# A macaron FFN–mixer–FFN layer on one core: TensorE in program order, streamed tiles moved by 64 bytes, other sums of squares

## The chip, the cores and the metric

The program runs on one core of one Trainium2 chip. The metric is the device time of one execution in microseconds (us), as a median of several runs. One profiled execution is read beside it; a group of rows is quoted word for word further down, and line numbers such as L351 are those of the kernel before.

## What is computed

One layer and a final norm, over 1024 tokens of width 1024 in float32, with a feed-forward width of 2816:

```
x = x + 0.5 * SwiGLU_1(RMSNorm(x))
x = x + W_out concat[ GLA heads(RMSNorm(x)), short-conv groups(RMSNorm(x)) ]
x = x + 0.5 * SwiGLU_2(RMSNorm(x))
out = RMSNorm(x)

rmsnorm(x, g):  x * rsqrt(mean(x * x) + 1e-6) * g
swiglu(x):      (silu(x @ w_gate) * (x @ w_up)) @ w_down
```

## The kernel before, in words

**Layout.** x lies transposed in SBUF as eight tiles of 128 channels by 1024 tokens, and the tokens are taken in two halves of 512 columns. Each operand of a product is split into two reduced float32 parts, high and low (`split`: a cast on ScalarE, then a subtraction on VectorE), and each product is three passes on TensorE (high by high, high by low, low by high), so that nearly all of TensorE's work is matmuls of 128x128 weights by 512 columns.

**FFN.** The 2816 hidden channels are 22 blocks f of 128 (gate and up together). Blocks 0 and 1 are done by `plain` as ordinary products. Blocks 2 to 21 go through a scheme of seven products in place of eight (`ups`, in the order u1, u5, u6, u2, u7, u3, u4; 12 matmuls each), and after each even f the pair of blocks before it is multiplied into x by `down` (D1, D2, D6, D3, D7, D5, D4). One period, two `ups` and one `down`, is 7x12x2 + 84 = 252 matmuls; each FFN has ten. The streamed right operands of `ups` are tiles named R (R11, R12, R21, R22 and S1, in pools with the tag R or h) and S (S2, S3, S4, in a pool of their own, `side`); of the seven products of one `ups` four stream an R tile and three an S tile, so 72 matmuls of a period have the form `ps<-S,w`. Sums between the products run on VectorE: after u7, `add(V, u1, ...)` (the row `act<-ps,p`, L88) reads the PSUM bank into which u4 then goes on accumulating, so u4 can start only behind it. The last pair is multiplied by `down_last` (L601), over ranges of tokens, and after each block d of a range the callback `after(n, d)` takes the square for the next norm.

**Weights** come in by DMA on SyncE's queue and are split by ScalarE and VectorE, some after a sum on GpSimd; `pump`, `free` and `need` move these steps along as room comes free, and `tick` and `spawn` place the norm's steps, written as generators, between the products by a count of TensorE's time.

**Norm.** `Norm.add(k)` squares a tile on ScalarE and adds it to a running sum; `stat` is four small matmuls (L314) that sum over the partitions, `fin` makes the reciprocal root (pow on GpSimd, L328), a diagonal `dg` on VectorE (L331), the broadcast matmul `rb` (L335), and, with `keep`, a copy of it to SBUF. `raw` (L342) multiplies x by gain and root. n1 and n3 are the norms ahead of the FFNs, n2 that ahead of the mixer, n4 the last one, which has three ranges in `tail`: 512, 256 and 256 tokens.

**Seams.** Seam 1 is the stretch from the first `down_last` to the mixer's first projections (`alr`, L709, and `pj`, L691), seam 2 that from the mixer's output projection (`dn`, L996) to the second `plain` (L461).

**Order.** A scheduler orders each engine's instructions by its own priorities within the dependences. `in_order(since)` adds dependences that keep every engine to program order; before, it is called once, at the start, over the first half of the first norm.

**Addresses.** Pools are laid one behind the other. By their sizes S3, S4 and S2 begin at 101376, 117760 and 134144 bytes in each partition, which are multiples of 128, as is the mixer's tile `o` of the second half. R, h, act, w and the mixer's `z` begin 64 bytes over a multiple of 128.

Of the kernel before, what the change touches and what calls it, by code (L numbers as in the profile page):

```python
# [16 lines left out]
P = 128  # L17
# [38 lines left out]
def trunk(ctx: ExitStack, tc: tile.TileContext, a, out):  # L56
# [220 lines left out]

    def rstd_of(ss, n):

        ms = tiny.tile([P, 4], F32, tag="ms", name=nm("ms"))  # L280
        G.tensor_scalar_add(ms[:, :n], ss[:, :n], EPS)
        r = tiny.tile([P, 4], F32, tag="rs", name=nm("rs"))
        G.tensor_tensor(r[:, :n], ms[:, :n], nhalf[:, :n], op=ALU.pow)
        return r

    class Norm:


        def __init__(self, c, w=HALF, engines="VGVGVVV"):
            self.c, self.w, self.n, self.engines, self.sums = c, w, w // P, engines, []  # L290
# [9 lines left out]
        def add(self, k):  # L300

            q, sums = self.square(k), self.sums
            two = "V" in self.engines
            if k < 1 + two:
                sums.append(q)
                return
            i = k % 2 if two and k < 6 else 0
            add(V if self.engines[k - 1] == "V" else G, sums[i], sums[i], q)
            if two and k == 6:
                add(V, sums[0], sums[0], sums.pop())  # L310
# [5 lines left out]
        def fin(self, bank, st=None, keep=True):  # L316

            n = self.n
            ss = tiny.tile([P, 8], F32, tag="st", name=nm("ss"))
            if st is None:  # L320
                t = bank("st")
                self.stat([t[:, 2 * j:2 * j + 2] for j in range(n)], self.sums[0], True, True)
                V.tensor_scalar_add(ss[:, 0:2 * n], t[:, 0:2 * n], EPS)
            else:
                for j in range(n):
                    V.tensor_scalar_add(ss[:, 2 * j:2 * j + 2], st[j], EPS)
            r = tiny.tile([P, 4], F32, tag="rs", name=nm("rs"))
            G.tensor_tensor(r[:, :n], ss.rearrange("p (j c) -> p j c", c=2)[:, :n, 0], nhalf[:, :n], op=ALU.pow)  # L328
            yield 4.0
# [3 lines left out]
            yield 1.5  # L333
# [3 lines left out]
            if keep:  # L337
                self.r = t2("rb")[:, :self.w]
                S.copy(self.r, rp)

# [16 lines left out]
    class Ffn:  # L357
# [81 lines left out]
        def half1_end(self):  # L439
            for q in range(2):  # L440
                self.right(("S3", "S4")[q], ("S3", "S4")[q])
                for k in range(4):
                    self.part(("S3", "S4")[q], k, self.raws[q, k])
            self.raws.clear()
# [6 lines left out]
        def plain(self):  # L451
            for n in range(2):
                for f in range(2):
                    pss = [self.bank(4 * n + 2 * f + m) for m in range(2)]
                    for q in range(2):
                        lts = [need(((self.i, "f", f), f"L{m + 1}{q + 1}")) for m in range(2)]
                        for k, rk in enumerate(self.r_of(f"R{q + 1}{n + 1}")):
                            for m in range(2):
                                for t, (i, j) in enumerate(PASSES):
# [3 lines left out]
                                                     stop=(q == 1 and k == 3 and t == 2))  # L463
                        if q:
# [6 lines left out]
                        tick(5.44)  # L471
# [112 lines left out]
        def down_last(self, after, ranges):  # L584
# [5 lines left out]
            for n, (c, w) in enumerate(ranges):  # L590
                h, o = divmod(c, HALF)
                for d in range(KT):
# [12 lines left out]
                    after(n, d)  # L605
                    tick(1.36 * w / HALF)
            free("wo", 4)


        def run(self, after, shut, ranges):  # L610
            self.plain()
            for _ in self.side:
                pass
            self.half1_end()
# [9 lines left out]
            shut()  # L624
            self.down_last(after, ranges)
# [381 lines left out]
    def norm_h(norm, h, bank):  # L1007

        yield from norm.fin(bank)
# [9 lines left out]
    def in_order(since):  # L1019

        prev = {}
        for i in nc.cur_bb.bb.instructions[since:]:
            if i.engine in prev:
# [3 lines left out]
        return len(nc.cur_bb.bb.instructions), prev  # L1027
# [32 lines left out]
    st = [f1.bank(4 + j)[:, 0:2] for j in range(4)]  # L1060
# [7 lines left out]
    pump(2)  # L1068
    pump(2)
# [3 lines left out]
    start = in_order(0)  # L1073
    for k in range(KT):
        nc.sync.dma_start(out=xh(k, 1), in_=a["x"][k * P:(k + 1) * P, HALF:T])
    nc.sync.dma_start(out=w_a1, in_=a["w_a1"])
# [148 lines left out]
```

## Time and profile before

| | before |
|---|---|
| median of 3 runs (lowest, highest) | 1829.99 us (1827.4, 1830.26) |
| the profiled execution | 1829.83 us |
| its span, first to last instruction | 1828.0 us, so 1.83 us lie around it |
| TensorE's mean granted clock | 0.983 of full speed |
| VectorE, ScalarE, GpSimd busy | 77%, 45%, 36% of the span |
| loads of weights and x | 107 MB, 61 GB/s over the span |

A row of the timeline or of a group names line, engine, operation and tiles (out<-in), then how many; in brackets stands the idle time before it and what ended that. Matmuls overlap in the pipeline, so the step from one start to the next tells what a matmul costs, and the printed duration (some 390 ns) does not.

### The profile page before, as it was taken

The page shows a single profiled execution, that of the slowest core. Times are in us where ns is not written, and L with a number is a line of the kernel's source. Part 1 is how long each engine was busy: PE and PEld are TensorE (multiplying, and loading weights), DVE is VectorE, ACT ScalarE, POOL GpSimd, SP SyncE. Part 2 cuts the span into 40 slices and gives each one's busy share as a digit, 9 for nine tenths or more (in the row PEclk, how much of TensorE's full clock was granted, in tenths as well). Part 3 has the DMA queues.
Part 4 walks back from the last instruction along what each step waited for, and adds up shares of the span by engine and source line. Part 5 has one row for each costly group of instructions (what it writes and reads, how often), then busy time and mean ns, then how long its engine had stood idle before and what let it go on. Part 6 is the DMA issues. An engine that isn't in the chain of part 4 may idle for free.

```text
span 1828.0 us, 20978 instructions
## 1 busy us (share of the span) xinstructions
PE 1761.6 (96%) x7830; PEld 1431.9 (78%) x7830; DVE 1405.9 (77%) x1822; ACT 814.3 (45%) x1432; POOL 650.1 (36%) x441
## 2 busy tenths in 40 slices
PE   8899999999999997899999999999999999999995
PEld 6678877878778876688888887877877887787874
DVE  4687888878887886666655668797888788887887
ACT  4354444544454453523343444454445444454442
POOL 2442445335442445120120121343544244533531
PEclk9899999999999998999999999999999999999997
DMA  5002111111112121222222222111111212111102
GB/s 187 24 24 70 52 63 48 46 58 58 47 46 70 49 73 35 69 84 84 76 78 84 93 70 81 43 39 58 58 47 47 70 48 65 50 47 58 58 24 92
DMA packets 35302, 112.92 MB, mean 62 GB/s; under 512 B 4576, under 2 KB 7040, under 8 KB 35200
## 3 DMA queue, kind: packets, MB, share of 16 engines
q1 hardware_dynamic: 35200, 111.58, 18.4%
q8 instruction: 61, 1.00, 0.2%
q14 instruction: 41, 0.34, 0.1%
HBM read 107.37 MB, written 4.19 MB: 61 GB/s over the span
## 4 chain that ended last, share of the span: by engine, by line
PE 68%; DVE 25%; issue 2%; POOL 2%; ACT 2%; DMA 0%; ACTq 0%; DVEq 0%; POOLq 0%
PE ps L351 37%; PE pj L691 11%; DVE x L519 8%; DVE act L85 5%; PE dn L996 5%; DVE w L85 5%; PE ps L581 3%; PE ps L461 2%; PE ps L601 2%; PE v L746 2%; DVE T L85 2%; POOL hraw L85 2%; DVE hraw L342 2%; PE sc L815 1%; PE ps L314 1%
## 5 line engine op out<-in xcount | busy, mean ns | idle before, releaser
L351 PE MATMUL ps<-R,w 128*128 128x512 f32 x1920 | 463.4, 391 | 3.0 <-DVE w L85 2.4
L351 PEld LDWEIGHTS ps<-R,w 128*128 128x128 f32 x1920 | 358.7, 188 | 88.3 <-DVE w L85 11.4
L581 PE MATMUL ps<-act,w 128*128 128x512 f32 x1680 | 400.2, 391 | 7.6 <-ACT ps L550 7.6
L581 PEld LDWEIGHTS ps<-act,w 128*128 128x128 f32 x1680 | 313.8, 188 | 81.2 <-ACT ps L550 16.0
L351 PE MATMUL ps<-S,w 128*128 128x512 f32 x1440 | 352.1, 397 | 4.1 <-ACT ps L493 4.1
L85 DVE TENSOR_TENSOR w<-raw,w 128x512 fp32r<-128x512 f32 x316 | 292.1, 926 | 54.0 <-ACT w L92 53.9
L351 PEld LDWEIGHTS ps<-S,w 128*128 128x128 f32 x1440 | 271.6, 189 | 71.0 <-ACT ps L493 5.0
L85 POOL TENSOR_TENSOR raw<-raw 128x512 f32<-128x512 f32 x60 | 78.4, 1307 | 642.4 <-DVE w L85 642.4
L92 ACT CAST w<-raw 128x512 fp32r<-128x512 f32 x316 | 194.9, 619 | 165.7 <-POOL raw L85 92.8
L88 POOL TENSOR_TENSOR x<-x,dx 128x512 f32<-128x512 f32 x160 | 264.1, 1686 | 7.2 <-ACT dx L568 7.2
L519 DVE SCALAR_TENSOR_TENSOR x<-ps,x 128x512 f32<-128x512 f32 x320 | 207.1, 684 | 49.3 <-PE ps L581 49.3
L691 PE MATMUL pj<-h,whi 128*128 128x512 f32 x640 | 201.9, 396 | 0.0
L85 DVE TENSOR_TENSOR wlo<-raw,whi 128x1024 fp32r<-128x1024 f32 x64 | 82.3, 1285 | 89.1 <-PE pj L691 52.8
L691 PEld LDWEIGHTS pj<-h,whi 128*128 128x128 f32 x640 | 119.7, 190 | 26.6 <-issue 1.9
L85 DVE TENSOR_TENSOR w<-T,w 128x512 fp32r<-128x512 f32 x120 | 118.3, 986 | 22.0 <-ACT w L92 22.0
L218 ACT CAST whi<-raw 128x1024 fp32r<-128x1024 f32 x64 | 67.0, 1047 | 138.1 <-PE pj L691 79.8
L691 PE MATMUL pj<-h,wlo 128*128 128x512 f32 x320 | 125.4, 392 | 0.0
L92 ACT CAST w<-T 128x512 fp32r<-128x512 f32 x120 | 74.3, 619 | 94.3 <-DVE T L85 56.2
L85 DVE TENSOR_TENSOR act<-act,act 128x512 fp32r<-128x512 f32 x98 | 103.2, 1054 | 13.5 <-ACT act L92 13.5
L92 ACT CAST act<-act 128x512 fp32r<-128x512 f32 x98 | 61.1, 626 | 116.6 <-DVE act L505 64.8
L85 DVE TENSOR_TENSOR T<-raw,raw 128x512 f32<-128x512 f32 x60 | 63.2, 1054 | 55.8 <-POOL raw L85 55.8
L85 POOL TENSOR_TENSOR raw<-raw,raw 128x512 f32<-128x512 f32 x60 | 97.9, 1631 | 4.7
(170 smaller groups left out, 2137.5 us busy)
## 6 DMA issues: line engine op xcount, KB each, us to landing
raw<-in_ffn_w SPq DMA_DIRECT2D x88, 512.0 KB, 3.5
raw<-in_ffn_wd SPq DMA_DIRECT2D x44, 512.0 KB, 3.5
raw<-in_w_fm SPq DMA_DIRECT2D x40, 512.0 KB, 3.4
raw<-in_w_out SPq DMA_DIRECT2D x16, 512.0 KB, 3.4
x<-in_x SPq DMA_DIRECT2D x16, 256.0 KB, 5.7
raw<-in_w_v SPq DMA_DIRECT2D x8, 512.0 KB, 3.4
out<-y SPq DMA_DIRECT2D x8, 256.0 KB, 2.1
out<-y SPq DMA_DIRECT2D x16, 128.0 KB, 2.0
```

Source lines behind the costliest of these rows:

```text
L85: eng.tensor_tensor(o, x, y, op=ALU.subtract)
L88: eng.tensor_tensor(o, x, y, op=ALU.add)
L92: S.copy(hi, src)
L218: S.copy(st[1], st[0])
L342: V.scalar_tensor_tensor(o, self.x(k), gains[:, g, k:k + 1], self.r, op0=ALU.mult, op1=ALU.mult)
L351: nc.tensor.matmul(ps, lt[:, c:c + P], rk[j], start=(start and n == 0), stop=(n == last), skip_group_check=True)
L461: nc.tensor.matmul(pss[m], lts[m][:, c:c + P], rk[j], start=(q == 0 and k == 0 and t == 0), stop=(q == 1 and k == 3 and t == 2))
L519: V.scalar_tensor_tensor(xh(d, n), ps, 0.5, xh(d, n), op0=ALU.mult, op1=ALU.add)
L581: nc.tensor.matmul(ps, l2[i], r[0][j], start=(start and n == 0), stop=(n == 2), skip_group_check=True)
L601: nc.tensor.matmul(ps, l2[i], rts[h][q][:, 512 * j + o:512 * j + o + w], start=(q == 0 and k == 0), stop=(q == 1 and k == 2))
L691: nc.tensor.matmul(pss[f], w[i][:, k, f * P:(f + 1) * P], h[j][:, 4 * kh + k, :], start=(kh == 0 and k == 0 and n == 0), stop=(kh == 1 and ...
L996: nc.tensor.matmul(pss[j], w[p][:, f * 512 + j * P:f * 512 + (j + 1) * P], act[q][i][:, f * 512:(f + 1) * 512], start=(i == 0 and f == 0 a ...
```

## The change

It has four parts. A tile `pad` of 64 bytes is laid ahead of the `side` pools, so that all S tiles and the mixer's o tiles begin 64 bytes later. TensorE's instructions of each FFN, from `plain` to ahead of `down_last`, are kept to program order, and from `down_last` to the seam's end (the end of the program in the second FFN) all four engines are; the start's range in program order takes in the squares of the second half. The sums of squares are made otherwise: n1's first half on VectorE in place of 32 small matmuls on TensorE (64 records in the profile), n2's first half by two chains on VectorE and GpSimd in place of one on GpSimd, the last range of n4 on VectorE; n2's first half reads its root from PSUM without a copy, and `norm_h` splits each tile one step behind. At the end results are stored as pairs of tiles, on SyncE's and ScalarE's queues in turn, the first range is scaled by ScalarE and GpSimd, the others by VectorE.

```diff
+    ctx.enter_context(tc.tile_pool(name="pad", bufs=1)).tile([P, 16], F32, name="pad")
...
     class Norm:
-        def __init__(self, c, w=HALF, engines="VGVGVVV"):
+        def __init__(self, c, w=HALF, chain=None):
...
             q, sums = self.square(k), self.sums
-            two = "V" in self.engines
-            if k < 1 + two:
+            if k < 1 + (self.chain is None):
                 sums.append(q)
...
+            elif self.chain:
+                add(self.chain, sums[0], sums[0], q)
+            else:
+                i = k % 2 if k < 6 else 0
+                add((V, G)[i], sums[i], sums[i], q)
...
-        def fin(self, bank, st=None, keep=True):
+        def fin(self, bank, keep=True, waits=(2.7, 1.3), fill=lambda: None):
...
     def run(self, after, shut, ranges):
+            since = here()
             self.plain()
             for _ in self.side:
                 pass
-            self.half1_end()
+            spawn(self.half1_end())
...
             shut()
+            in_order(since, nc.tensor)
+            self.end = here()
             self.down_last(after, ranges)
...
     def norm_h(norm, h, bank, keep=True):
-        for k in range(KT):
-            raw = t2("hraw")
-            norm.raw(raw, 1, k)
-            split(raw, hi[:, k, :], lo[:, k, :])
-            if k % 2:
-                yield 2.7
+        prev = None
+        for k in range(KT + 1):
+            if k < KT:
+                raw = t2("hraw")
+                norm.raw(raw, 1, k)
+            if prev is not None:
+                split(prev, hi[:, k - 1, :], lo[:, k - 1, :])
+                yield 1.3
+            prev = raw
...
-    n1 = [Norm(0), Norm(HALF, engines="GGGGGGG")]
-    n2 = [Norm(0, engines="GGGGGGG"), Norm(HALF, engines="GGGGGGG")]
+    n1 = [Norm(0, chain=V), Norm(HALF, chain=G)]
+    n2 = [Norm(0), Norm(HALF, chain=G)]
...
-    n4 = [Norm(*r) for r in tail]
+    n4 = [Norm(*tail[0]), Norm(*tail[1]), Norm(*tail[2], chain=V)]
...
     for k in range(KT):
-        n1[0].stat(st, n1[0].square(k), k == 0, k == KT - 1)
-    begin = n1[0].fin(f1.bank_norm, st, False)
+        n1[0].add(k)
+    begin = n1[0].fin(f1.bank_norm, False)
...
     for k, _ in enumerate(f1.half0(n1[0])):
         if k >= 4:
             pump(1)
-    start = in_order(0)
+        n1[1].add(k)
+    f1.start = in_order(0, nc.tensor, V, S, G)
...
-            spawn(norm_h(n2[0], hm[0], f1.bank_norm))
+            spawn(norm_h(n2[0], hm[0], f1.bank_norm, False), 4.0)
     f1.run(to_mix, eh.close, halves)
     finish()
+    in_order(f1.end, nc.tensor, V, S, G)
...
+    def first():
+        yield from n4[0].fin(f2.bank_norm)
+        for k in range(0, KT, 2):
+            y = room("wr", "y")
+            for i in range(2):
+                xg, yv = t2("xg"), y[:, i * HALF:(i + 1) * HALF]
+                S.mul(xg, n4[0].x(k + i), gains[:, 3, k + i:k + i + 1])
+                G.tensor_tensor(yv, xg, n4[0].r, op=ALU.mult)
+            store(0, k, y.rearrange("p (i c) -> p i c", i=2))
+            yield 1.3
...
     f2.run(last, eh.close, tail)
     finish()
+    in_order(f2.end, nc.tensor, V, S, G)
```

**In the layers**, this is TensorE before, over the last two `ups` of an FFN (f odd, then f even): a row is a line, the bank written, the right operand and the weights.

```order
L351 MATMUL ps_4729<-R_189,w_4652 128x512 x11
L351 MATMUL ps_4650<-R_394,w_4631 128x512 x12
L351 MATMUL ps_4729<-R_189,w_4652 128x512
L351 MATMUL ps_4747<-R_493,w_4673 128x512 x12
L351 MATMUL ps_4742<-S_75_494,w_4690 128x512 x12
L351 MATMUL ps_4729<-R_205,w_4708 128x512 x12
L351 MATMUL ps_4781<-S_79_580,w_4726 128x512 x12
L351 MATMUL ps_4742<-S_80_589,w_4744 128x512 x12
L581 MATMUL ps_4881<-act_4792,w_4783 128x512 x3
L581 MATMUL ps_4875<-act_4792,w_4783 128x512 x3
L351 MATMUL ps_4781<-R_394,w_4762 128x512 x12
L581 MATMUL ps_4881<-act_4795,w_4819 128x512 x3
```

Changed, the same place; here `R_332` is the operand of u4, as `R_394` is above:

```order
L354 MATMUL ps_4129<-S_88_627,w_4131 128x512 x12
L354 MATMUL ps_4168<-R_332,w_4149 128x512 x12
L354 MATMUL ps_4247<-R_175,w_4170 128x512 x12
L354 MATMUL ps_4265<-R_404,w_4191 128x512 x12
L354 MATMUL ps_4260<-S_65_405,w_4208 128x512 x12
L354 MATMUL ps_4247<-R_199,w_4226 128x512 x12
L354 MATMUL ps_4299<-S_79_575,w_4244 128x512 x12
L354 MATMUL ps_4260<-S_88_627,w_4262 128x512 x12
L354 MATMUL ps_4299<-R_332,w_4280 128x512 x12
L588 MATMUL ps_4393<-act_4310,w_4301 128x512 x3
L588 MATMUL ps_4399<-act_4310,w_4301 128x512 x3
```

Before, u4 of the odd f stands behind 11 matmuls of the next u1, and u4 of the even f behind six of D1; now each follows u3 at once.

**At the start**, VectorE before; `ss` is the sum with epsilon, `dg` the diagonal:

```order
L326 TENSOR_SCALAR ss_162<-ps_110 128x2
L326 TENSOR_SCALAR ss_162<-ps_111 128x2
L326 TENSOR_SCALAR ss_162<-ps_112 128x2
L326 TENSOR_SCALAR ss_162<-ps_113 128x2
L85 TENSOR_TENSOR w_169<-raw_106,w_169 128x512
L85 TENSOR_TENSOR w_172<-raw_106,w_172 128x512
L331 TENSOR_TENSOR dg_175<-ident,rs_167 128x512
```

Changed, the same place:

```order
L88 TENSOR_TENSOR sq_114<-sq_114,sq_116 128x512
L88 TENSOR_TENSOR sq_114<-sq_114,sq_119 128x512
L88 TENSOR_TENSOR sq_114<-sq_114,sq_122 128x512
L88 TENSOR_TENSOR sq_114<-sq_114,sq_125 128x512
L88 TENSOR_TENSOR sq_114<-sq_114,sq_128 128x512
L88 TENSOR_TENSOR sq_114<-sq_114,sq_131 128x512
L88 TENSOR_TENSOR sq_114<-sq_114,sq_134 128x512
L327 TENSOR_SCALAR ss_142<-ps_137 128x8
L85 TENSOR_TENSOR w_146<-raw_110,w_146 128x512
L85 TENSOR_TENSOR w_149<-raw_110,w_149 128x512
L333 TENSOR_TENSOR dg_152<-ident,rs_144 128x512
```

Seven additions of squares on VectorE have come ahead of `ss`, which is one instruction now, and of the first weights' subtractions.

**At seam 1**, TensorE before, from the last matmuls of `down_last` (L601) to the mixer's first:

```order
L601 MATMUL ps_5393<-act_5191,w_5145 128x512 x3
L601 MATMUL ps_5393<-act_5290,w_5162 128x512 x3
L335 MATMUL ps_5349<-dg_5325,ones 128x512
L709 MATMUL alr_5465<-h_5353,wa_5461 128x512
L691 MATMUL pj_5485<-h_5353,whi_5182 128x512
L691 MATMUL pj_5486<-h_5353,whi_5182 128x512
L314 MATMUL st_5518<-ones,sq_5301 128x2 x4
L709 MATMUL alr_5465<-h_5354,wa_5461 128x512
L709 MATMUL alr_5465<-h_5353,wa_5461 128x512
L691 MATMUL pj_5485<-h_5354,whi_5182 128x512
L691 MATMUL pj_5485<-h_5353,wlo_5404 128x512
L691 MATMUL pj_5486<-h_5354,whi_5182 128x512
```

Changed, the same place; the four small matmuls of the first half's `stat` stand further up, with four rows of L608 between:

```order
L608 MATMUL ps_5321<-act_5168,w_5122 128x512 x3
L608 MATMUL ps_5321<-act_5258,w_5139 128x512 x3
L337 MATMUL ps_5332<-dg_5319,ones 128x512
L608 MATMUL ps_5342<-act_5168,w_5122 128x512 x3
L608 MATMUL ps_5342<-act_5258,w_5139 128x512 x3
L608 MATMUL ps_5357<-act_5168,w_5122 128x512 x3
L608 MATMUL ps_5357<-act_5258,w_5139 128x512 x3
L608 MATMUL ps_5372<-act_5168,w_5122 128x512 x3
L608 MATMUL ps_5372<-act_5258,w_5139 128x512 x3
L720 MATMUL alr_5440<-h_5334,wa_5436 128x512
L720 MATMUL alr_5440<-h_5335,wa_5436 128x512
L720 MATMUL alr_5440<-h_5334,wa_5436 128x512
```

The broadcast `rb` (`ps<-dg,ones`) stood behind the last matmul of `down_last` and now has six rows, 18 matmuls, of it behind; the `stat` of the second half, which stood among the first projections, has left this stretch for a place some 40 rows on, and thirteen `alr` matmuls, those of the first six blocks of h and one of the seventh, come ahead of the first `pj`.

## Rows read from the trace of the kernel before

**Rows 1.** The page, busy time and share of the span of each engine.

```profile
PE 1761.6 (96%) x7830; PEld 1431.9 (78%) x7830; DVE 1405.9 (77%) x1822; ACT 814.3 (45%) x1432; POOL 650.1 (36%) x441
```

**Rows 2.** Windows, first of four layer stretches: length, busy (instructions) by engine, clock.

```profile
430.00:488.80 58.80, 58.29 (x254) 47.08 (x252) 48.77 (x61) 27.53 (x50) 24.92 (x17) 1.00 0.17 54
```

**Rows 3.** Waits of TensorE in the four stretches: total us, times, longest.

```profile
PE ps L581 <- ACT ps L550: 1.4, 4, 0.4
PE ps L351 <- DVE w L85: 0.5, 3, 0.2
```

**Rows 4.** Timeline of TensorE in one period: start, duration, instructions.

```profile
438.31 8.34 PE L351 MATMUL ps<-R,w 128*128 128x512 f32 x36
446.49 2.96 PE L351 MATMUL ps<-S,w 128*128 128x512 f32 x12
449.29 2.90 PE L351 MATMUL ps<-R,w 128*128 128x512 f32 x12
452.03 5.76 PE L351 MATMUL ps<-S,w 128*128 128x512 f32 x24
457.63 1.54 PE L581 MATMUL ps<-act,w 128*128 128x512 f32 x6
```

**Rows 5.** Timeline of TensorE in the output projection, second half.

```profile
1111.81 0.39 PE L996 MATMUL dn<-z,wlo 128*128 128x512 f32 x1
...
1117.25 0.40 PE L996 MATMUL dn<-z,wlo 128*128 128x512 f32 x1
...
1118.82 0.39 PE L996 MATMUL dn<-o,wlo 128*128 128x512 f32 x1
...
1129.32 0.39 PE L996 MATMUL dn<-o,wlo 128*128 128x512 f32 x1
```

**Rows 6.** Timeline of VectorE in that period, the additions ahead of u4.

```profile
438.79 0.68 DVE L88 TENSOR_TENSOR act<-ps,p 128x512 f32<-128x512 f32 x1
...
457.34 0.68 DVE L88 TENSOR_TENSOR act<-ps,p 128x512 f32<-128x512 f32 x1
```

**Rows 7.** Timeline of all engines at the start.

```profile
4.12 13.81 PE L314 MATMUL ps<-ones,sq 128*128 128x2 f32 x64 [4.12 <-ACT sq L297]
...
7.15 3.35 ACT L297 ACTIVATE sq<-x 128x512 f32<-128x512 f32 x5 [0.30 <-DMA x<-in_x]
...
18.21 1.41 POOL L328 TENSOR_TENSOR rs<-ss,nhalf 128x4 f32<-128x4 f32 x1 [17.78 <-DVE ss L326]
...
23.96 2.50 PE L461 MATMUL ps<-R,w 128*128 128x512 f32 x5 [1.49 <-ACT R L92]
```

**Rows 8.** Windows, second norm and first products of FFN 1.

```profile
52.00:102.00 50.00, 40.53 (x152) 30.88 (x152) 38.93 (x57) 23.74 (x42) 22.78 (x11) 0.83 0.07 22
```

**Rows 9.** Windows, seam 1 from the end of `down_last` on.

```profile
699.10:731.00 31.90, 22.08 (x75) 16.25 (x74) 19.37 (x22) 10.16 (x16) 12.64 (x10) 0.73 0.10 34
```

**Rows 10.** Timeline of VectorE in seam 1.

```profile
693.25 3.68 DVE L604 SCALAR_TENSOR_TENSOR x<-ps,x 128x512 f32<-128x512 f32 x6 [0.85 <-PE ps L601]
...
698.56 2.37 DVE L85 TENSOR_TENSOR wlo<-raw,whi 128x1024 fp32r<-128x1024 f32 x1
700.85 1.75 DVE L331 TENSOR_TENSOR dg<-ident,rs 128x512 f32<-128x512 f32 x1
...
705.43 8.46 DVE L342 SCALAR_TENSOR_TENSOR hraw<-x,gains,rb 128x512 f32<-128x512 f32 x8 [2.24 <-ACT rb L339]
713.82 2.48 DVE L85 TENSOR_TENSOR h<-hraw,h 128x512 fp32r<-128x512 f32 x4
```

**Rows 11.** Windows, seam 2 with the first products of FFN 2.

```profile
1141.00:1221.00 80.00, 76.46 (x326) 61.42 (x327) 64.78 (x89) 38.32 (x69) 27.77 (x15) 0.98 0.12 40
```

**Rows 12.** The page, a group of GpSimd's: count | busy us, mean ns.

```profile
L88 POOL TENSOR_TENSOR x<-x,dx 128x512 f32<-128x512 f32 x160 | 264.1, 1686 | 7.2 <-ACT dx L568 7.2
```

**Rows 13.** Timeline at the end.

```profile
1819.58 1.22 PE L335 MATMUL ps<-dg,ones 128*128 128x256 f32 x2 [6.61 <-DVE y L342]
1820.84 3.22 DVE L342 SCALAR_TENSOR_TENSOR y<-x,gains,ps 128x256 f32<-128x256 f32 x8 [1.31 <-PE ps L335]
```

More of the change, by code (lines that the diff above doesn't have):

```diff
@@ L302, in add @@
             q, sums = self.square(k), self.sums
-            two = "V" in self.engines
-            if k < 1 + two:
+            if k < 1 + (self.chain is None):
                 sums.append(q)
[L306 to L310, printed above, removed]
+            elif self.chain:
[3 more added lines that the diff above has]
+                add((V, G)[i], sums[i], sums[i], q)
+                if k == 6:
+                    add(V, sums[0], sums[0], sums.pop())
         def stat(self, st, q, start, stop):
@@ L339, in fin @@
                 S.copy(self.r, rp)
+            fill()
         def raw(self, o, g, k):
@@ L1005, in out_proj, with norm_h, in_order @@
                     tick(5.44)
-    def norm_h(norm, h, bank):
-        yield from norm.fin(bank)
+    def norm_h(norm, h, bank, keep=True):
+        yield from norm.fin(bank, keep)
         hi, lo = (hp.tile([P, KT, HALF], F32R, tag="h", name=nm("h")) for _ in range(2))
         h += [hi, lo]
-        for k in range(KT):
-            raw = t2("hraw")
-            norm.raw(raw, 1, k)
-            split(raw, hi[:, k, :], lo[:, k, :])
-            if k % 2:
-                yield 2.7
-    def in_order(since):
-        prev = {}
+        prev = None
[7 more added lines that the diff above has]
+            prev = raw
+    def in_order(since, *engines):
+        prev, es = {}, [e.engine for e in engines]
         for i in nc.cur_bb.bb.instructions[since:]:
+            if i.engine not in es:
+                continue
             if i.engine in prev:
@@ L1067, in trunk @@
     next(begin, None)
-    pump(2)
-    pump(2)
+    pump(4)
+    for k in range(KT):
+        nc.sync.dma_start(out=xh(k, 1), in_=a["x"][k * P:(k + 1) * P, HALF:T])
+    nc.sync.dma_start(out=w_a1, in_=a["w_a1"])
     for k, _ in enumerate(f1.half0(n1[0])):
@@ L1072, in trunk, with second @@
             pump(1)
-    start = in_order(0)
-    for k in range(KT):
-        nc.sync.dma_start(out=xh(k, 1), in_=a["x"][k * P:(k + 1) * P, HALF:T])
-    nc.sync.dma_start(out=w_a1, in_=a["w_a1"])
-    def second(f, norm, squares=False):
-        if squares:
-            for k in range(KT):
-                norm.add(k)
-            yield 5.0
+        n1[1].add(k)
+    f1.start = in_order(0, nc.tensor, V, S, G)
+    def second(f, norm, wait):
+        yield wait
         yield from norm.fin(f.bank_norm)
         yield from f.half1(norm)
-    f1.start = start
-    f1.side = second(f1, n1[1], True)
+    f1.side = second(f1, n1[1], 8.0)
     spawn(f1.side)
@@ L1142, in last, with fill @@
             return
-        def rest():
-            yield from n4[n].fin(f2.bank_norm, keep=n == 0)
-            if n:
-                held.append(n)
-                if n == 2:
-                    for i in held:
-                        yield from store(i)
-            else:
-                yield from store(0)
-        spawn(rest())
+        if n == 0:
+            spawn(first(), 4.0)
+        elif n == 1:
+            spawn(second_range(), 2.6)
+        else:
+            finish()
+            ys = [y for k in range(0, KT, 2) for y in [scaled(1, k)] for _ in range(2)]
+            def fill():
+                for y in ys[:2]:
+                    next(y)
+                del ys[:2]
+            for _ in n4[2].fin(lambda s: f2.bank({"st": 0, "rb": 1}[s]), False, fill=fill):
+                pass
+            for k in range(0, KT, 2):
+                for _ in scaled(2, k):
+                    pass
+            fill()
     f2.run(last, eh.close, tail)
     finish()
+    in_order(f2.end, nc.tensor, V, S, G)
     ep.close()
```

55 lines of the change are left out of this document (33 added, 22 removed).

## The prediction, made before the changed kernel was run

> **What bounds the kernel now.** I read the page first: TensorE is busy for 96% of the span, every other engine for less than 78% [rows 1]. Then the windows: in the layers each period of 252 matmuls takes 58.8 us, at full clock, with TensorE busy for 58.3 [rows 2]. So two things can make the kernel faster: fewer nanoseconds for a matmul, or less time in which TensorE waits or runs at its lower clock. The windows at the ends show where that second kind lies. Between 52 and 102 us 152 matmuls took 50.0 us at a granted clock of 0.83 [rows 8]; between 699.1 and 731 us 75 took 31.9 at 0.73 [rows 9]; between 1141 and 1221 us 326 took 80.0 at 0.98 [rows 11]. The ends of the program add a stretch before the first product, at 23.96 [rows 7], and one after TensorE's last broadcast, at 1819.58 [rows 13].
>
> The profiled execution took 1829.83 us, 1.83 more than its span and 0.16 under the median; the sum is made against it. A measurement of this kernel can tell about 0.2%, 3.7 us, from no change.
>
> **The 64 bytes (layers).** Steps between the starts of matmuls, in one period: 36 that stream R in 8.18 us, from 438.31 to 446.49, are 227.2 ns each; 12 that stream S, to 449.29, are 233.3; 24 that stream S, from 452.03 to 457.63, are 233.3 [rows 4]. The same step shows in the output projection, where code and weights are alike: 24 with the operand z take 5.44 us, 226.7 ns each, and 45 with o take 10.50, 233.3 ns each [rows 5]. z and R begin 64 bytes over a multiple of 128, o and S on one. The trace can't say if it is the address modulo 128 or where in the memory the tile lies; I take the first, since o and S lie in different tiles and agree to 0.1 ns. Then 72 matmuls a period gain 6.1 ns: 0.44 us, 8.8 over 20 periods (ten in each FFN). The bounds are 0 and 8.8. Where a product hides work of VectorE, a shorter cover gives some of it back as waiting; I take 6.
>
> The Trainium skill ("TensorE: Matmul & The Clock Gate", section "Back-to-back issue gap") speaks against this part: by it the step between matmuls follows from the count of columns and the clock, which is about 216 ns for 512 columns. The trace agrees that steps are alike within a tile, and differs in that they are 227 or 233 ns by tile. By the rule this part would be worth 0.
>
> **TensorE in program order (layers).** At the steps above a period is 180 x 227.2 + 72 x 233.3 ns = 57.7 us; 1.1 of the 58.8 are waits and restarts. The waits that the profile names are those of `down` for ScalarE's copies and of `ups` for weights [rows 3], 0.5 us a period; a wait also stretches the next start, which is the rest. In the changed order D2 comes a whole D1 later, and weights are wanted in the order in which they are made, so I count both waits as gone: 1.1 a period.
>
> What is late next is u4, which has to follow u3 at once. Even f: u6 ends at 449.29 and the addition that frees u4's bank starts at 457.34 and takes 0.68 [rows 4, 6], so it is done 8.7 us after u6; three products at 227.2 ns cover 8.2. Wait: 0.5. D1 then reaches a bank that VectorE frees somewhat later; 0.2. Odd f: u3 ends at 438.31, the addition at 439.47 [rows 4, 6], so 1.2 late, if VectorE is then as far behind as now. It should be less so, as `down` no longer mixes with the next u1 and gives it its work earlier; between 0 and 1.2 I take 0.2. Sum 0.9, gain 0.2 a period, rounded down to 2 us over 20. Bounds: 1.1 x 20 = 22 gained if nothing waits; the loss is a rival below. The layers together: **8**.
>
> **Start.** The last square is done at 10.50, but 64 small matmuls fill 4.12 to 17.93, 0.216 us each; pow starts at 18.21, takes 1.41, and the first product comes 4.34 after it, at 23.96 [rows 7]. Changed, VectorE adds each square as it comes, the last at about 11.25 (an addition is 0.68 [rows 6]); 8 small matmuls at 0.216 end at 13.0; 0.3 to pow, 1.41, 4.34: 19.05. Gain 4.9. The second half's squares are added on GpSimd among the first products, not after them, so its norm comes early enough to spare most of the stretch at 52 to 102 us: 152 matmuls at 229 ns would be 34.8 of the 50.0, so 15.2 are lost there [rows 8]. One stall, of u7 for a copy, stays (4, with the clock); the second half's `stat`, now in fixed order among the first products, waits for GpSimd's chain, and the splits of the first half meet GpSimd's additions, which cost VectorE's a second read each (7). Gain 4 to 5. Start: **9**, between 5 and 16.
>
> **Seam 1.** 75 matmuls at 227.2 ns are 17.0 of 31.9 us, so 14.9 are to be had [rows 9]. I take little of it. rb follows `dg`, which ends at 702.60 behind a weight subtraction of 2.37 [rows 10]. In the new order `stat` is due after two blocks of the second range, but the second range must first wait about 2 us for the split of its own operand, which stands behind a square and an addition on ScalarE and VectorE; and the same subtraction still stands ahead of `dg`. By these durations rb comes about 3 us earlier, near 700. Reading it from PSUM spares the copy, so the first `hraw` starts near 701 in place of 705.43. Then thirteen `alr` matmuls stand ahead of the first projection, and they need six blocks of h and half of the seventh. Until these are split VectorE has seven `hraw` (8.46 / 8 = 1.06 each now, 0.67 where GpSimd doesn't read beside it, an estimate from 0.61 for an x block), six splits (0.62), three blocks of x (0.61) and one weight subtraction (1.3 to 2.37) [rows 10]: 11.5 to 15.3 us. The first `pj` starts between 712.5 and 716.3; 51 matmuls at 227.2 ns are 11.6, and the low clock, which such sparse matmuls bring with them [rows 9], costs some 2.5. So this point is reached at 726.6 to 730.4, where it was 731. Gain **3**, between 0 and 13.
>
> **Seam 2.** 326 matmuls at 229 ns are 74.7 of 80.0 us [rows 11], so 5.3 are lost. `stat` moves to a fixed place after 12 products and may wait for VectorE's sums by about as much as the later stalls shrink. **0**, between -4 and 5.
>
> **End.** The last range's rb waits 6.6 us for a bank, freed by the y of the range before, and starts at 1819.58; eight y follow to 1824.06 [rows 13]. Changed, it has a bank of its own, but its pow stands on GpSimd behind eight multiplications for the first range. The nearest row for one is 1.69 us [rows 12], 13.5 for eight; from about 1804.5 they end at 1818. pow (1.41 at most [rows 7]), `dg` and rb (1.22) and eight y (3.22) end at 1824; if a multiplication is 1.3, at 1821. The last store is as large and as late behind y as before, and on two queues. Gain **2.5**, between -2 and 7.
>
> **Sum.** 8 + 9 + 3 + 0 + 2.5 = 22.5; 1829.8 - 22.5 = **1807**.
>
> **Rivals.**
> *The pad does nothing* (the region, not the address, sets the step; the rule named above has this outcome). For it: S and o lie at higher addresses than R and z. Against: tiles of two kinds, one step [rows 4, 5]. Then 6 less: 1813.
> *The seams give what their windows hold.* If splits keep ahead of `alr`, seam 1 gives 13 and the start 12, 13 more: 1794. For it: 14.9 us to be had [rows 9]. Against: `hraw` at 1.06 [rows 10].
> *No wait is left in the layers.* 22 + 8.8 in place of 8: 1784. For it: VectorE is busy for 48.8 of 58.8 us [rows 2]. Against: the addition ends after u3 in both f [rows 4, 6].
> *u4 waits for VectorE's addition in both f.* Program order takes away the 11 and 6 matmuls that stand ahead of it now. If VectorE is as late as now [rows 6] or a little later, 1.2 us in each f and 0.25 at D1, 2.65 a period against 1.1, cost 31 over 20 periods; and the shorter S matmuls give nothing, since the chain through VectorE then sets the pace. 1829.8 - 14.5 + 31 = 1846. It decides from 0.7 us more a period than now, since 14.5 / 20 is what the other parts give. For it: both additions end after u3 today. Against: VectorE has 10 us free in a period [rows 2].
>
> **How the numbers follow.** The forecast has a chance of 0.45, the pad without effect 0.17, the seams in full 0.15, no waits 0.09, u4 waiting 0.14. Faster by over 0.2%: the first four, less 0.02 for a bad sum of bounds: 0.84. Of the last, 0.05 are waits of 0.6 to 0.9 that cancel the rest, within 0.2%, and 0.09 slower, to which the 0.02 are added. The range leaves out u4 waiting and most of the case without waits: 1788 to 1826.
>
> **What would show it.** Steps of 227 ns for S and for o (right) or 233 (wrong). No wait of L588 for copies, and a wait of u4's first matmul of about 0.5 in even f. First product near 19. In seam 1 `alr` waiting for h until about 714. In the end pow behind GpSimd's y. A period over 58.8 us would make the forecast wrong, one under 57.3 also.

## The result, and the profile after

The changed kernel takes 1817.85 us (median of 4 runs, 1815.78 to 1820.42) against 1828.7 beside it: ratio 0.9941, interval 0.9922 to 0.9960. It is faster, by 10.9 us where 22.5 were forecast, and lies inside the range. The profiled execution is one of 1820.42 us, with a span of 1818.6; two of the four runs are at 1816, and in profiles of later kernels with the same start u3 of f = 2 ends up to 3.5 us sooner than here (91.84 in run 10, 95.36 here).

The page after: TensorE's busy time and its three largest groups (mean ns of one matmul, then the idle time ahead of them).

```profile
PE 1743.9 (96%) x7774; PEld 1426.4 (78%) x7774; DVE 1377.7 (76%) x1825; ACT 830.1 (46%) x1439; POOL 649.6 (36%) x442
...
L354 PE MATMUL ps<-R,w 128*128 128x512 f32 x1920 | 455.5, 391 | 8.7 <-DVE act L88 8.6
...
L588 PE MATMUL ps<-act,w 128*128 128x512 f32 x1680 | 388.1, 391 | 0.0
...
L354 PE MATMUL ps<-S,w 128*128 128x512 f32 x1440 | 342.0, 391 | 3.0 <-ACT ps L493 3.0
```

The waits of `down` (L581 before, L588 now) for copies and those for weights [rows 3] are gone. In their place the next line, u4 (in `ps<-R,w`), waits 8.6 us for VectorE. These are TensorE's longest waits by line in the whole run (total, times, longest; the 12.7 us stand ahead of its first instruction):

```profile
PE ps L318 <- DVE sq L88: 18.4, 3, 12.7
PE ps L337 <- DVE dg L333: 15.9, 5, 5.8
PE ps L354 <- DVE act L88: 8.6, 19, 0.5
PE ps L608 <- ACT act L92: 7.9, 2, 4.2
```

To see where the time went, both traces are read at the same places. The end of u3 is the start of its last matmul and one step; the other places are starts of the matmul named.

| place | before | after | stage gained |
|---|---|---|---|
| first product | 23.96 | 20.56 | 3.4 |
| end of u3, f = 2, FFN 1 | 104.81 | 95.36 | 6.1 |
| end of u3, f = 21, FFN 1 | 673.53 | 657.06 | 7.0 |
| 48th `pj` matmul of the mixer | 730.75 | 720.03 | -5.8 |
| last `dn` matmul | 1140.52 | 1128.21 | 1.6 |
| end of u3, f = 2, FFN 2 | 1207.99 | 1197.72 | -2.0 |
| end of u3, f = 21, FFN 2 | 1777.57 | 1759.76 | 7.5 |
| last matmul of `down_last` | 1804.32 | 1796.99 | -10.5 |
| end of the span | 1828.02 | 1818.65 | 2.0 |

Start and layers together gained 24 us, and 18 of it was given back in the two stretches behind the layers and in seam 2. The profiled execution is the slowest of the four, so the stages sum to 9.4 where the medians differ by 10.9.

**Layers.** TensorE's timeline in one period after, u7 and u3 (S), u4 (R), then `down`:

```profile
438.26 5.60 PE L354 MATMUL ps<-S,w 128*128 128x512 f32 x24
444.31 3.06 PE L354 MATMUL ps<-R,w 128*128 128x512 f32 x12 [0.45 <-DVE act L88]
447.20 19.40 PE L588 MATMUL ps<-act,w 128*128 128x512 f32 x84
```

From the start of the 24 matmuls with S to that of u4 it is 6.05 us; at 227 ns they take 5.45, and the wait of u4, 0.45, with the restart makes the rest. Before, the same 24 took 5.60 with nothing behind them that waited [rows 4]. Nine even blocks lie between the ends of u3 at f = 4 and f = 20 (163.66 and 634.02 before, 153.20 and 618.00 after): eight periods of 58.80 before and 58.10 after.

**Start.** The small matmuls and the first product after, and the window that answers to [rows 8]:

```profile
12.67 1.86 PE L318 MATMUL ps<-ones,sq 128*128 128x2 f32 x8 [12.67 <-DVE sq L88]
...
20.56 10.08 PE L466 MATMUL ps<-R,w 128*128 128x512 f32 x31 [1.49 <-ACT R L92]
```

```profile
52.00:102.00 50.00, 46.90 (x193) 37.58 (x192) 43.49 (x54) 22.30 (x41) 22.59 (x12) 0.93 0.10 31
```

In the same 50 us TensorE now does 193 instructions where it did 152.

**Seam 1.** TensorE after, from the first range of `down_last` (L608) to the mixer:

```profile
660.46 11.14 PE L608 MATMUL ps<-act,w 128*128 128x512 f32 x48
675.28 4.60 PE L608 MATMUL ps<-act,w 128*128 128x512 f32 x9 [3.68 <-ACT act L92]
679.68 1.70 PE L318 MATMUL ps<-ones,sq 128*128 128x2 f32 x8
...
689.84 1.13 PE L337 MATMUL ps<-dg,ones 128*128 128x512 f32 x2 [2.54 <-DVE dg L333]
...
702.50 4.47 PE L720 MATMUL alr<-h,wa 128*128 128x512 f32 x7 [1.99 <-ACT h L92]
```

Of these 48 matmuls 45 are the first range's last ones and three the second range's first, at 670.76 to 671.21. Then TensorE stands still for about 4 us, until 675.28, and 9 matmuls take until 679.68, at a granted clock of 0.50. The broadcast waits 2.5 us for `dg`. It starts 32.8 us after the end of u3, where before it was 29.1:

```profile
702.65 2.07 PE L335 MATMUL ps<-dg,ones 128*128 128x512 f32 x2 [3.50 <-DVE dg L331]
```

VectorE in the first range shows why:

```profile
665.55 0.69 DVE L88 TENSOR_TENSOR sq<-sq,sq 128x512 f32<-128x512 f32 x1 [0.70 <-ACT sq L300]
...
668.26 1.16 DVE L88 TENSOR_TENSOR sq<-sq,sq 128x512 f32<-128x512 f32 x1 [0.70 <-ACT sq L300]
...
671.33 2.13 DVE L88 TENSOR_TENSOR sq<-sq,sq 128x512 f32<-128x512 f32 x2 [0.70 <-ACT sq L300]
673.37 0.69 DVE L611 SCALAR_TENSOR_TENSOR x<-ps,x 128x512 f32<-128x512 f32 x1
674.75 0.69 DVE L88 TENSOR_TENSOR sq<-sq,sq 128x512 f32<-128x512 f32 x1 [0.70 <-ACT sq L300]
675.36 0.68 DVE L85 TENSOR_TENSOR act<-act,act 128x512 fp32r<-128x512 f32 x1
```

In each of the four rows of additions of squares (`sq<-sq,sq`) it has first waited 0.70 us for ScalarE's square, which itself waits for the block of x just ahead of it on VectorE. Before the change GpSimd made these additions, and VectorE did six blocks of x in a row:

```profile
682.14 3.68 DVE L604 SCALAR_TENSOR_TENSOR x<-ps,x 128x512 f32<-128x512 f32 x6 [1.85 <-PE ps L601]
...
687.36 0.69 DVE L604 SCALAR_TENSOR_TENSOR x<-ps,x 128x512 f32<-128x512 f32 x1 [0.67 <-PE ps L601]
```

With three such stalls ahead of it the last block of x starts 2.8 us after its last matmul did (673.37 after 670.53); before it was 0.4 (687.36 after 686.93). The fourth stands between that block and the split. The split of the second range's operand, which program order puts behind that block and its square, ends at 676.04.

**Seam 2.** The `stat` of the second norm now has a fixed place, behind 12 matmuls, and waits there:

```profile
1135.46 1.87 PE L318 MATMUL ps<-ones,sq 128*128 128x2 f32 x8 [4.14 <-DVE sq L88]
```

**End.** The same wait for an operand as at seam 1, then TensorE's wait for the second range's `dg`; below it ScalarE and VectorE at that moment:

```profile
1778.15 0.58 PE L608 MATMUL ps<-act,w 128*128 128x256 f32 x1 [4.18 <-ACT act L92]
...
1803.09 1.19 PE L337 MATMUL ps<-dg,ones 128*128 128x256 f32 x2 [5.82 <-DVE dg L333]
```

```profile
1799.97 0.42 ACTq L1149 DMA_DIRECT2D out<-y  x1
1800.49 0.42 ACT L300 ACTIVATE sq<-x 128x256 f32<-128x256 f32 x1 [2.87 <-POOL y L1170]
```

```profile
1800.94 0.43 DVE L88 TENSOR_TENSOR sq<-sq,sq 128x256 f32<-128x256 f32 x1 [3.69 <-ACT sq L300]
```

A store on ScalarE's queue waits for GpSimd's products of the first range (2.87 us), ScalarE's square of the last range stands behind it, and VectorE waits 3.69 us for that square with the later blocks of x and `dg` behind. At this end VectorE added squares of the first range before the change too, and its rows there name no wait for ScalarE; so here it is not the place of the sums that is new, but their order.

### The profile page after: what moved, and what is told of

It reads as the page before. It is cut to its first block, busy times and chain, and to the rows that moved or that the text cites. A ratio compares the mean times of both kernels' runs of the same rounds, so it can differ in the third digit from the quotient of the medians.

```text
span 1818.6 us, 20907 instructions
## 1 busy us (share of the span) xinstructions
PE 1743.9 (96%) x7774; PEld 1426.4 (78%) x7774; DVE 1377.7 (76%) x1825; ACT 830.1 (46%) x1439; POOL 649.6 (36%) x442
## 4 chain that ended last, share of the span: by engine, by line
PE 47%; issue 21%; POOL 18%; DVE 11%; ACT 2%; DMA 0%; POOLq 0%; SPq 0%; ACTq 0%; DVEq 0%
PE ps L588 16%; POOL x L88 12%; PE pj L702 12%; PE ps L354 5%; PE dn L1007 5%; POOL raw L85 4%; DVE S L85 2%; PE v L757 2%; DVE S L88 2%; POOL hraw L85 2%; PE ps L608 2%; PE sc L826 1%; DVE hraw L345 1%; DVE sq L88 1%; DVE T L85 1%
## 5 line engine op out<-in xcount | busy, mean ns | idle before, releaser
L354 PE MATMUL ps<-R,w 128*128 128x512 f32 x1920 | 455.5, 391 | 8.7 <-DVE act L88 8.6
L588 PE MATMUL ps<-act,w 128*128 128x512 f32 x1680 | 388.1, 391 | 0.0
L588 PEld LDWEIGHTS ps<-act,w 128*128 128x128 f32 x1680 | 313.8, 188 | 71.2 <-DVE act L512 6.5
L354 PE MATMUL ps<-S,w 128*128 128x512 f32 x1440 | 342.0, 391 | 3.0 <-ACT ps L493 3.0
L85 DVE TENSOR_TENSOR w<-raw,w 128x512 fp32r<-128x512 f32 x316 | 278.4, 887 | 77.3 <-ACT w L92 77.3
L85 DVE TENSOR_TENSOR T<-raw,raw 128x512 f32<-128x512 f32 x60 | 48.7, 812 | 55.7 <-POOL raw L85 55.7
```

The source lines that it names most:

```text
L85: eng.tensor_tensor(o, x, y, op=ALU.subtract)
L354: nc.tensor.matmul(ps, lt[:, c:c + P], rk[j], start=(start and n == 0), stop=(n == last), skip_group_check=True)
L588: nc.tensor.matmul(ps, l2[i], r[0][j], start=(start and n == 0), stop=(n == 2), skip_group_check=True)
```

## The experiments

Theory after the result: the pad and the order on TensorE give what the layers gained, and what was lost behind the layers is the program order on VectorE and ScalarE, not the new sums, stores or TensorE's order. Rivals: the sums and stores themselves, or TensorE's order. All times are medians; each run has its own kernels before beside it, at 1828.5 to 1829.1.

**1. The pad alone** (`e1_pad_only`): the kernel before, with

```diff
+    ctx.enter_context(tc.tile_pool(name="pad", bufs=1)).tile([P, 16], F32, name="pad")
```

> The kernel before with the 64-byte pad alone. Theory (address modulo 128 sets the step of a streamed tile): matmuls that stream S and o go from 233 to 227 ns, 1440 x 6.5 ns = 9.4 us and 64 x 6.5 = 0.4 us for o, less what the layers give back by waiting: 7 to 10 us less than before. Rival (the step hangs on something else that the change did, for instance the new order of the matmuls): steps stay at 233 ns and the time within 2 us of before.

Measured 1815.86, ratio 0.9931 (0.9918 to 0.9943): 12.6 us less than before, more than expected. Its page shows products with R and with S alike now, a printed duration of 391 and 392 ns, where S had 397, and so do the steps in its timeline:

```profile
L353 PE MATMUL ps<-R,w 128*128 128x512 f32 x1920 | 461.8, 391 | 3.1 <-DVE w L85 2.3
...
L353 PE MATMUL ps<-S,w 128*128 128x512 f32 x1440 | 342.9, 392 | 5.0 <-ACT ps L495 5.0
```

```profile
445.48 2.88 PE L353 MATMUL ps<-R,w 128*128 128x512 f32 x12
448.20 5.60 PE L353 MATMUL ps<-S,w 128*128 128x512 f32 x24
453.64 1.52 PE L583 MATMUL ps<-act,w 128*128 128x512 f32 x6
```

24 with S take 5.44 us from start to start, 226.7 ns each, where they took 5.60 [rows 4]. The 12 with R behind a run of S gain too: 2.72 us here, 2.74 before. Matmul by matmul, the first five behind a run of S took 226, 236, 229, 232 and 231 ns before (means over some 80 such places) and take 227 each here, so each of the four such places in a period gains 20 ns. 72 x 6.6 + 4 x 20 ns are 0.56 us, nearly all that the period lost: it is 58.22 us (eight periods between 162.53 and 628.33). This one line alone is worth about as much as the whole change.

**2. The change without the pad** (`e2_no_pad`).

> The changed kernel without the pad. Theory: 7 to 10 us slower than the changed kernel, so 1 to 4 us under before. If program order makes the layers depend on VectorE, part of the pad's gain is hidden there and taking it away costs less, 4 to 6 us.

Measured 1824.17, ratio 0.9975 (0.9965 to 0.9986): 6.3 us slower than the changed kernel. So with the rest of the change about half of the pad's gain is hidden. Part of that is u4, which waits 5.5 us in all without the pad and 8.6 with it; the rest was not followed. This trace also tells what the step hangs on. TensorE in the first products of FFN 2, groups of 24 with the operands named (streamed, weights):

```profile
1163.08 5.76 PE L465 MATMUL ps<-S,w 128*128 128x512 f32 x24
1168.68 5.62 PE L465 MATMUL ps<-R,w 128*128 128x512 f32 x24
1174.14 5.62 PE L465 MATMUL ps<-S,S 128*128 128x512 f32 x24
1179.59 5.68 PE L465 MATMUL ps<-R,S 128*128 128x512 f32 x24
1185.11 5.16 PE L353 MATMUL ps<-R,w 128*128 128x512 f32 x22
```

From start to start: S with w 5.60 us, R with w 5.46, S with S 5.45, R with S 5.52. Here S begins on a multiple of 128 and R and w 64 bytes over one. The same streamed S costs 233 ns with weights that begin otherwise and 227 with weights that begin alike. So it is neither the region nor the streamed address alone: what these four and run 1 have in common is that the step is short where the two operands agree.

**3. No order behind the layers** (`e3_no_seam_order`).

```diff
-    in_order(f1.end, nc.tensor, V, S, G)
...
-    in_order(f2.end, nc.tensor, V, S, G)
```

> The changed kernel without program order of the four engines at the two places behind the layers (seam 1 and the end); the order in the layers and at the start stays. Theory (program order puts each square's addition ahead of the next blocks of x on VectorE, which then waits for ScalarE, and puts the split of the second range's operand last): the 4 us waits of the last products for their operand go, with the low clock behind them, 5 to 8 us at seam 1 and 5 to 9 at the end, 10 to 16 us under the changed kernel, near 1804. Rival (the loss comes from the new sums and stores themselves): within 3 us of the changed kernel.

Measured 1799.06, ratio 0.9842 (0.9829 to 0.9856): 18.8 us under the changed kernel. Seam 1 turns from a loss of 5.8 into a gain of 4.4 (48th `pj` at 710.27, u3 at 657.42). The new sums and stores are not what lost these 18.8 us.

**4. The order in the layers alone** (`e4_layers_order_only`): the kernel before, with `in_order(since, nc.tensor)` from `plain` to ahead of `down_last`.

> The kernel before with TensorE kept to program order in both FFNs from plain to ahead of down_last, nothing else. Theory: the period loses the waits for copies and weights and gains one of 0.6 us for u4 of the even f, some 0.25 us less a period, 4 to 6 us less than before in all. Rival (without the other changes u4 waits in both f): 10 to 30 us slower than before.

Measured 1837.9, ratio 1.0049 (1.0036 to 1.0062): 9.4 us slower than before, which neither expectation had. The layers did as the theory says: 3.3 and 4.2 us less between the ends of u3 of f = 2 and f = 21, a period of 58.47. But program order also fixes the second norm's `stat` among the first products, and there TensorE waits for a chain of additions on GpSimd:

```profile
48.99 1.87 PE L314 MATMUL ps<-ones,sq 128*128 128x2 f32 x8 [10.23 <-POOL sq L88]
```

The loss is 10 us by f = 2 in FFN 1 and 2.8 more at seam 2. In the change this stall is 0.31 us. There the second half's squares are added among the first products, which fits; no run took that part away by itself.

**5. Only TensorE in order behind the layers** (`e5_pe_only_seams`): `in_order(f1.end, nc.tensor)` and the same for f2.

> The changed kernel with only TensorE kept to program order behind the layers; VectorE, ScalarE and GpSimd are free there. Theory (VectorE's order costs the time, not TensorE's): most of the 18.8 us that freeing all four gave come back, 1799 to 1805. Rival (TensorE's fixed order costs it, as products of the second range can't be drawn ahead of those of the first): 1812 to 1818.

Measured 1797.53, ratio 0.9827 (0.9814 to 0.9840). TensorE's own order costs nothing here (run 3, without it, is at 1799.06); the other three engines' order costs the 20.3 us. They were not freed one by one. TensorE in seam 1:

```profile
672.36 2.12 PE L608 MATMUL ps<-act,w 128*128 128x512 f32 x8 [0.48 <-DVE act L85]
674.96 1.05 PE L318 MATMUL ps<-ones,sq 128*128 128x2 f32 x8 [0.48 <-DVE sq L88]
...
681.40 1.13 PE L337 MATMUL ps<-dg,ones 128*128 128x512 f32 x2 [1.18 <-DVE dg L333]
...
686.49 1.65 PE L720 MATMUL alr<-h,wa 128*128 128x512 f32 x5
```

The operand is 0.48 late, not 4, and `dg` 1.2.

**6. The operand's split earlier** (`e6_operand_early`), all orders kept:

```diff
-                    if n == 1 and d == 0:
-                        rts[1][1] = operand("ao", "act", r22)
...
+                    if n == 0 and d == KT - 1:
+                        rts[1][1] = operand("ao", "act", r22)
```

The new place is ahead of the last block's update of x.

> The changed kernel, all orders kept, with the split of the second range's operand written ahead of the last block's update of x and its square. Theory: the 4.1 and 4.2 us waits of the last products for that operand shrink under 1 us and the low clock behind them goes with them: 8 to 12 us under the changed kernel, 1806 to 1810. Rival (the lag of VectorE behind the blocks of x costs it in any case, the wait only moves to the broadcast): under 4 us.

Measured 1811.6, ratio 0.9906 (0.9892 to 0.9919): 6.3 us less, between the two. The wait is 2.0 us in two parts, and VectorE's lag is still there, and `dg` is as late as ever:

```profile
669.59 0.50 PE L606 MATMUL ps<-act,w 128*128 128x512 f32 x1 [0.26 <-ACT act L92]
671.85 2.09 PE L606 MATMUL ps<-act,w 128*128 128x512 f32 x8 [1.76 <-DVE act L85]
...
682.08 2.07 PE L337 MATMUL ps<-dg,ones 128*128 128x512 f32 x2 [2.96 <-DVE dg L333]
```

**7. The squares two blocks behind x** (`e7_squares_behind`), with 6, all orders kept:

```diff
-                    after(n, d)
+                    behind_x.append((n, d))
+                    if len(behind_x) > 2:
+                        after(*behind_x.pop(0))
...
```

The squares left over are taken behind the loop, and the norm's steps, which the last square starts, begin 2.7 us (at seam 1) or 1.3 to 1.4 us (at the end) sooner after it, so that they keep their places among the products.

> As the kernel with the early operand, and each square and its addition written two blocks behind the update of x, so that VectorE need not wait for ScalarE; all orders kept. Theory (not order as such costs the time, but this order): 12 to 18 us under the changed kernel, 1800 to 1806, about as good as no order. Rival (any fixed order loses): not better than the early operand alone by over 2 us.

Measured 1802.89, ratio 0.9858 (0.9844 to 0.9871): 15.0 us less. All 57 matmuls, 45 of the first range and 12 of the second, go through without a wait for the operand:

```profile
658.05 13.36 PE L607 MATMUL ps<-act,w 128*128 128x512 f32 x57
673.39 1.05 PE L318 MATMUL ps<-ones,sq 128*128 128x2 f32 x8 [1.98 <-DVE sq L88]
...
681.41 1.13 PE L337 MATMUL ps<-dg,ones 128*128 128x512 f32 x2 [1.13 <-DVE dg L333]
```

VectorE makes the same additions, and none waits for ScalarE. So program order on VectorE is not bad as such: the order written down was, and with two blocks between a block of x and its square it loses little.

**8. All stores on SyncE's queue** (`e8_stores_sp`).

> The changed kernel with all stores issued on SyncE's queue, none on ScalarE's. Theory: ScalarE's last squares no longer stand behind a store that waits for GpSimd, where VectorE waited 3.7 us for them: 2 to 4 us under the changed kernel, 1814 to 1816. Rival (stores then queue up on one engine, or GpSimd's results come as late anyhow): within 1 us.

Measured 1815.54, ratio 0.9927 (0.9915 to 0.9940): 2.3 us less; ScalarE's squares no longer stand behind a store. The runs of the two kernels overlap (1813.6 to 1817.6, 1815.8 to 1820.4), but the traces agree on the place: from the last matmul of `down_last` to the end of the span it is 19.4 us here and 21.7 in the change.

**9. No order in the layers** (`e9_no_layer_order`): the change without `in_order(since, nc.tensor)`.

> The changed kernel without program order of TensorE in the layers; start, seam 1 and end keep theirs. Theory: the waits for copies and weights come back, so a period costs about 0.2 us more and the whole 3 to 5 us more than the changed kernel; seam 2, where stat is then free to wait, gives 2 to 4 back: 1817 to 1821. Rival (the order in the layers costs time, as it did alone): 1805 to 1814.

Measured 1820.66, ratio 0.9952 (0.9939 to 0.9964): 2.8 us slower by the medians, though the runs overlap. The traces show both parts, as expected: the waits for copies are back (7.6 us), the period is 58.26 and the layers are 4.9 us longer; seam 2 is 3.6 us better up to u3 of f = 2.

**10. Seam 2's `stat` later** (`e10_seam2_later`): as 5, with `second(f2, n3[1], 5.0)` for 0.0.

> The kernel with only TensorE in order behind the layers, and the second FFN's second norm placed 5 us later between the first products, so that TensorE meets its stat when the sums are ready. Theory (the 4.1 us wait of that stat and the low clock behind it are what seam 2 lost): 3 to 5 us under that kernel, 1792.5 to 1794.5. Rival (its broadcast then comes too late for the second half's products): within 1 us.

Measured 1793.61, ratio 0.9808 (0.9795 to 0.9822): 3.9 us under 5; in the two traces seam 2 is 3.0 us shorter. Behind 30 matmuls, where it was 12, `stat` has nothing to wait for:

```profile
1120.05 1.05 PE L318 MATMUL ps<-ones,sq 128*128 128x2 f32 x8
```

This is the best kernel of the study, 24 us under the change.

**11. Another end** (`e11_new_end`): as 10, the first range's results made after the last sums, half on GpSimd and half on VectorE, all stores on SyncE's queue, and ScalarE and GpSimd in order from the second `down_last` on. At seam 1 they stay free, unlike what the expectation and its rival say. The new end goes against what VectorE shows in 5, where three last additions take 3.96 us beside GpSimd's multiplications:

```profile
1779.04 3.96 DVE L88 TENSOR_TENSOR sq<-sq,sq 128x256 f32<-128x256 f32 x3
```

> The kernel with the later stat, and another end: the first range's results are made after the last sums, half on GpSimd and half on VectorE, all stores on SyncE, and ScalarE and GpSimd in program order behind the layers. Theory (the last additions of squares cost VectorE 1.2 to 1.5 us each because GpSimd's multiplications run beside them, 0.4 without): the last stat 4 us earlier, 3 to 5 us under the kernel with the later stat, 1788 to 1791. Rival (program order of ScalarE and GpSimd at seam 1 costs as much as it gives): 1792 to 1798.

Measured 1794.42 (1791.37 to 1798.95), ratio 0.9811 (0.9797 to 0.9825): no better. The last additions do take 0.42 us each now. From the last matmul of `down_last` to the end it takes 20.0 us, 1.5 less than in 10, but the stretch ahead of it, from the end of u3, is 2.8 longer, and there, with ScalarE in order, the second range waits for its operand again:

```profile
PE ps L608 <- ACT act L92: 1.7, 1, 1.7
```

**12. The first sums on TensorE** (`e12_start_sums_on_pe`): the change with 32 small matmuls again for the first half of the first norm.

> The changed kernel with the first norm's sums made by 32 small matmuls on TensorE again. Theory: the first product comes 3.4 us later, and what follows waits with it: 3 to 5 us slower than the changed kernel, 1821 to 1823. Rival (the start's gain comes only from the second half's squares): within 1 us of the changed kernel.

Measured 1820.89, ratio 0.9958 (0.9945 to 0.9970): 3.0 us slower, its first product at 24.53 (20.56 in the change).

## Why the prediction was right and wrong

**Right.** The direction; the wait of u4 of the even f, 0.5 forecast and 0.45 measured; a period between 57.3 and 58.8, 58.10; no waits for copies or weights in the periods. The odd f's u4 does not wait at all, where I took 0.2. All four rivals fell. The pad has its effect (runs 1, 2). The rule of the Trainium skill ("TensorE: Matmul & The Clock Gate", section "Back-to-back issue gap") that was weighed against it, a step that follows from columns and clock alone, about 216 ns here, does not agree with these traces: they have 227 and 233. (The section calls this the gap of an isolated matmul and gives about 131 ns for a stream with weight loads; no trace here shows that either.) That u4 waits in both f, the rival on the slower side, did not happen. One wait is left, so the layers are not without any. And seam 1 did not give what its window holds.

**Right in part by luck.** The start: 9 forecast and 9.5 measured to the end of u3 of f = 2, but the first product came 3.4 earlier, not 4.9 (`stat` begins at 12.67, where the last addition was to be done at 11.25), and the second half gave 6.1, not 4 to 5. The tail behind the last matmul: 2.5 forecast and 2.0 measured. pow does stand right behind GpSimd's y there (it starts at 1808.37, the last two y at 1805.92, for 2.50), but the tail also holds the store's stall of 3.7 us, which the sum did not have; its 1824 leaves 0.15 us for `dg`, which takes 0.42. And with the stretch ahead of the last matmul taken in, the new end gave nothing: from the end of u3 to the end of the span it is 50.45 us before, 58.9 in the change and 50.4 in run 5, which has the new end and no order on the other engines.

**Wrong: the layers, mis-sized.** Forecast 8, measured 14.5 (7.0 and 7.5). I took 6 of 8.8 for the pad and 2 for the order (0.2 a period is 4 over 20, of which I kept 2). By the periods, the order gives 0.33 a period without the pad (58.80 to 58.47) and 0.12 with it (58.22 to 58.10), the pad 0.58 without the order and 0.37 with it; together 0.70, 14 us. The pad's term was too small: alone it made 0.58 x 20 = 11.6, above my upper bound of 8.8, since S goes to 226.7 ns and not 227.2, and the five matmuls behind each run of S, which I had read as steps of R, get faster with it (run 1).

**Wrong: "the second range must first wait about 2 us for the split of its own operand", and the end without such a wait.** This step failed. I took VectorE to be as far along as before when the last block of x is done, and added the instructions that now stand ahead of the split. I had not followed VectorE's new order through the whole first range. There each addition stands right behind the block of x whose square it needs, so VectorE waits for ScalarE 0.70 us, four times, and the delay adds up. The wait is 4 us with 4 to 5 us at half the clock behind it (granted 0.50), and it comes at both places. The broadcast, which I had 3 us earlier, comes 3.7 later by the end of u3. Seam 1: 3 forecast, -5.8 measured; the last range: not counted, -10.5 measured. Runs 3 and 5 show that these engines' order is the cause (18.8 and 20.3 us), run 7 that it is the place of the squares and additions in it (15.0 with the operand's split earlier, which alone is 6.3, run 6).

**Wrong: seam 2.** 0 forecast, -2.0 measured: the wait of `stat` was named (VectorE's sums), 4.1 us, but what I set against it, later stalls that shrink, is smaller. Run 10 shows the price, 3.9 by the medians and 3.0 in the seam itself.

**Not in the prediction:** stores on ScalarE's queue hold the last squares, 3.7 us in the trace and 2.3 by run 8. I had the two queues only as harmless.

What stays open: which of the three engines' orders costs how much; whether order would cost as much at seam 1 with the sums on GpSimd, as they were; 2.2 of the 10.5 us of the last range, which run 5 does not give back; and why the granted clock falls in some runs and not in others behind the wait of u6 of f = 2 near 80 us. That wait, for a copy by ScalarE, is where the prediction had one of u7; it is 2.9 to 3.0 us in the profiles of the change, run 7 and run 10 alike, and the granted clock from 76 to 96 us is 0.83 in the first and 1.00 in the other two. The four runs of the change itself have mean clocks of 0.981 to 0.986 and differ by 4.6 us.

## What to carry to other kernels

Behind the layers, fixing program order on the engine that bounds the kernel cost nothing here; fixing it on the engines that feed it made each cross-engine round trip in the written order a stall, which two blocks of distance removed. Follow such an order through the whole stretch, not only at the place that waits at the end. And an order that pays in the layers can lose more at the one norm whose sums are late, so each fixed small matmul needs its inputs' time worked out.

## What the runs showed of the hardware that was not expected

In these traces the step of a 512-column matmul goes by whether the streamed operand and the weights begin alike modulo 128 bytes: 227 ns where they do (R with w 5.46 / 24, S with S 5.45 / 24), 230 to 233 ns where they differ by 64 bytes (R with S 5.52 / 24, S with w 5.60 / 24), all four in a row of one trace (run 2). Moving the pools behind the pad by 64 bytes was worth 12.6 us, 0.7%, in a kernel of 1828 us. Only these two offsets occur here; no other was tried, so that it is 128 bytes that count, and not a larger power of two, is not shown.
